# A two-layer encoder in split fp32: the gate and up products of one block of 128 output columns, ordered high parts first and low parts after

## The chip, the cores and the metric

The kernel runs on 1 core of one Trainium2 chip. The metric is device time: the median of 3 runs is 616.48 us (616.14 to 616.51). The engines are named as in the profile: PE (TensorE matmul), PEld (TensorE weight load), DVE (VectorE), ACT (ScalarE), POOL (GpSimd), SP (SyncE, which only issues DMAs here).

## The reference

Two layers of an encoder over 256 tokens of 1024 channels. Each layer has a mixer (three kinds of attention side by side) and a channel sublayer. Only the second one is touched here:

```python
D_MODEL, SEQ, DEPTH, D_FF = 1024, 256, 2, 2816
def channel_sublayer(x, n2, w_gu, cw, cb, w_dn):
    h = rms_norm(x, n2)
    g, u = jnp.split(h @ w_gu, 2, axis=-1)
    g = depthwise_conv_centred(g, cw, cb)        # along the tokens, 3 taps
    return x + (jax.nn.gelu(g, approximate=False) * u) @ w_dn
```

All tensors are float32. `h @ w_gu` is 256 x 1024 by 1024 x 5632.

## The kernel before

**Split numbers.** TensorE multiplies in the faster fp32r form. To keep accuracy, every operand is split into a high part (its fp32r rounding) and a low part (what is left). A product is then three products: high by high, low by high, high by low.

**Units of weights.** Weights come in units of at most 128 x 2048 values, 51 a layer. `load` (L581) brings a unit into one of four `raw` buffers by a DMA from SP's queue. `split` (L607) makes the two parts chunk by chunk: ACT casts a chunk of 512 columns into `wp_hi`, DVE subtracts and writes `wp_lo`; there are two buffers of each (`PARTS`). `unit` (L625) hands out the next unit and first records the loads four units ahead and the splits two units ahead.

**Gate and up.** `h2` (L1244, `act_hT` in the profile) holds the normalised input, transposed: for each of 8 groups of 128 channels the 256 tokens' high parts and beside them their 256 low parts. `half_up` (L1259) makes 256 output columns of gate or up from one unit. For each of its two blocks of 128 columns (`j`) it takes one PSUM bank (`psw_w`, four banks) of 128 x 512, and for each of 8 channel groups (`k`) `part` issues two matmuls: `wh` against all 512 columns of `h2[:, k]` (128x512: both tokens' parts at once), and `wl` against the 256 columns of the tokens' high parts (128x256, added to the first half of the bank). In the text the first is a wide product, the second a narrow one. Each has its own weight load. `joined` adds the bank's two halves: ACT copies the second half out, DVE adds the first. With `first=True`, the first gate unit of a layer, the order is written out by hand, because half of `h2` is still being made then.

**What follows.** `gate` (L1305) scales, convolves and applies GELU; `up` (L1324) multiplies and splits the result into `act_ch` and `act_cl`; `down` (L1334) multiplies these with `w_down` in 24 matmuls of 128x512 a unit, into four accumulators that stay in PSUM through the layer (`psa_a`). The sequence `FFN` (L74) is G0 U0 G1 D0 U1 G2 D1 U2 ... G10 U10 D9 D10. In layer 0, steps 4 to 9 also split the output projection's weights of layer 1 (`keep`, L565, tiles `act_mixT`) and store them to DRAM, and steps 2 to 4 make tables for layer 1.

**Order on the engines.** The code does not issue instructions directly: it records operations with a rank (its place in the program, plus some hundred for work that may come later). `order` (L303) then plays a list schedule: at each step it takes the ready operation that could start first by its own model of durations (`cost`, L416: an fp32r matmul of n columns is n / 2.4 + 2.5 ns), ties going to the lower rank, and this fixes each engine's instruction order. So a change of order in the program can shift neighbours on other engines. All instructions are issued from one place (L413), so the profile has L413 on every row, and groups are told apart by tiles.

Of the kernel before, what the change touches and what calls it, by code (L numbers as in the profile page):

```python
# [18 lines left out]
P = 128  # L19
# [3 lines left out]
KD = D // P  # L23
# [432 lines left out]
def encoder_kernel(  # L456
# [21 lines left out]
    nc = Plan(tc)  # L478
# [146 lines left out]
    def unit():  # L625

        i = taken[0]
        taken[0] += 1
        with nc.later(SPLIT_LATER):
            while len(raws) < min(i + AHEAD + RAWS - PARTS, len(views)):  # L630
                load(len(raws))
            while len(parts) < min(i + AHEAD, len(views)):
                split(len(parts))
        return parts[i]
# [14 lines left out]
    def split_T(srcs, hi, lo, k0, g, name):  # L649


        n = g.shape[1]
        for b in range(0, n, 2):
            m = min(2, n - b)
            ps = psw.tile([P, 2, S], F32, tag="w", name=f"pt_{name}_{b}")
            for i in range(m):
                k = b + i
                for t in range(NT):
                    nc.tensor.transpose(
                        ps[:, i, t * P : (t + 1) * P], srcs[t][:, k * P : (k + 1) * P], ident  # L660
                    )
            for i in range(m):
                k = b + i
                h, o = hi[:, k0 + k], lo[:, k0 + k]
                nc.scalar.activation(h, ps[:, i], AF.Copy, scale=g[:, k : k + 1])
                nc.vector.scalar_tensor_tensor(
                    o, ps[:, i], g[:, k : k + 1], h.bitcast(F32), ALU.mult, ALU.subtract
                )

    def halves(h):  # L670
        return [xs[:, t, h * 512 : (h + 1) * 512] for t in range(NT)]
# [144 lines left out]
    for l in range(DEPTH):  # L816
# [427 lines left out]
        h2 = act.tile([P, KD, 2, S], F32R, tag="hT", name=f"h2{l}", bufs=1)  # L1244
        h2_hi, h2_lo = h2[:, :, 0], h2[:, :, 1]
# [13 lines left out]
        def half_up(name, first=False):  # L1259

            wh, wl = unit()
            ps = [psw.tile([P, 2, S], F32, tag="w", name=f"{name}{j}") for j in range(2)]

            def part(j, k):
                js = slice(j * P, (j + 1) * P)
                nc.tensor.matmul(ps[j], wh[:, k, js], h2[:, k], start=k == 0, stop=False)
                nc.tensor.matmul(ps[j][:, 0], wl[:, k, js], h2_hi[:, k], start=False, stop=k == KD - 1)

            if first:
                for j in range(2):  # L1270
                    part(j, 0)
                split_T(halves(1), h2_hi, h2_lo, 4, gains[:, 2, l, 4:8], f"n2{l}1")
                for j in range(2):
                    for k in range(1, 4):
                        part(j, k)
                for k in range(4, KD):
                    part(0, k)
                for k in range(4, KD):
                    part(1, k)
                row_scale()  # L1280
                return ps
            for j in range(2):
                for k in range(KD):
                    part(j, k)
            return ps

        def row_scale():

            for t in range(NT):
                nc.tensor.transpose(  # L1290
                    rps[:, t * P : (t + 1) * P], r2[:, t : t + 1].to_broadcast([P, P]), ident
                )
            nc.vector.tensor_copy(rb, rps[:, :S])
# [11 lines left out]
        def gate(s):  # L1305
            nm = f"{l}_{s}"
            Gs = joined(half_up(f"G{nm}", s == 0), f"Gs{nm}")
            nc.vector.tensor_tensor(Gs, Gs, rb.unsqueeze(1).to_broadcast([P, 2, S]), op=ALU.mult)
            A = act.tile([P, 2, S], F32, tag="s2k", name=f"A{nm}", bufs=NS2K)
            for j in range(2):  # L1310
                f = 2 * s + j
                col = lambda i: cw[:, 22 * i + f : 22 * i + f + 1]
                nc.scalar.activation(A[:, j], Gs[:, j], AF.Identity, bias=col(3), scale=col(1))
                nc.vector.scalar_tensor_tensor(
                    A[:, j, 1:S], Gs[:, j, 0 : S - 1], col(0), A[:, j, 1:S], ALU.mult, ALU.add
                )
                nc.vector.scalar_tensor_tensor(
                    A[:, j, 0 : S - 1], Gs[:, j, 1:S], col(2), A[:, j, 0 : S - 1], ALU.mult, ALU.add
                )
            B = act.tile([P, 2, S], F32, tag="s2k", name=f"B{nm}", bufs=NS2K)  # L1320
            nc.scalar.activation(B, A, AF.Gelu)
            made[s] = B

        def up(s):  # L1324
            nm = f"{l}_{s}"
            C = joined(half_up(f"U{nm}"), f"C{nm}")
            nc.vector.tensor_tensor(C, made[s], C, op=ALU.mult)
            ch = act.tile([P, 2, S], F32R, tag="ch", name=f"ch{nm}", bufs=2)
            cl = act.tile([P, 2, S], F32R, tag="cl", name=f"cl{nm}", bufs=2)
            nc.scalar.copy(ch, C)  # L1330
            nc.vector.tensor_tensor(cl, C, ch.bitcast(F32), op=ALU.subtract)
            ready[s] = (ch, cl)
# [114 lines left out]
```

## Time and profile before

The profiled execution took 616.62 us, of which the span from its first to its last instruction is 614.9 us.

| | |
|---|---|
| median of the runs | 616.48 us |
| profiled execution, its span | 616.62 us, 614.9 us |
| granted TensorE clock, mean | 0.999 |
| HBM traffic | 196 GB/s over the span |
| DMA from `w_gate_up` | 44 issues of 1024 KB, 5.1 us to landing |

How to read it: a matmul's row in the timeline gives its start, and a duration that includes the time in the pipeline; since matmuls overlap, the pace is the distance from one start to the next, not the duration. A timeline row merges neighbours of the same kind (x2). PEld rows are weight loads; they overlap the matmuls. The clock times in the rows are counted from the span's start.

### The profile page before, as it was taken

The numbers are of one execution on the slowest core, as the hardware profiler recorded it, in microseconds if no ns is written. First come the engines' busy times: TensorE is split into PE (matmuls) and PEld (weight loads), VectorE is DVE, ScalarE is ACT, GpSimd is POOL, SyncE is SP. The second block draws the span as 40 slices with busy tenths as digits, with TensorE's granted clock in tenths as the row PEclk, the third lists the DMA queues.
The fourth block names the chain that finished last, engine by engine and source line by source line (L and its number), as shares of the span: only waits on it lengthen the run. The fifth ranks groups of instructions, "written<-read, shape, count | busy, mean of one in ns | idle before, by whom it ended". The sixth has DMA issues, their size and how long they took to land.

```text
span 614.9 us, 9864 instructions
## 1 busy us (share of the span) xinstructions
PE 605.8 (99%) x3484; PEld 523.8 (85%) x3484; DVE 487.4 (79%) x1000; ACT 428.1 (70%) x1064; POOL 82.5 (13%) x136
## 2 busy tenths in 40 slices
PE   8999999999999999999999999999999999999997
PEld 6998878888888888888899988887888888888885
DVE  4898989897777988887867797867977777777774
ACT  6788989686566676666588898866755656556651
POOL 2731230211400000000022212332000000000000
PEclk9999999999999999999999999999999999999999
DMA  8794312655596999978444744553565556555501
GB/s 279 273 290 156 102 36 86 227 191 194 169 244 237 366 350 325 312 272 277 154 151 153 243 136 173 201 179 119 200 228 174 173 202 203 173 176 202 187 20 68
DMA packets 85073, 121.44 MB, mean 198 GB/s; under 512 B 9864, under 2 KB 69608, under 8 KB 85024
## 3 DMA queue, kind: packets, MB, share of 16 engines
q1 hardware_dynamic: 82752, 112.17, 55.3%
q0 software_dynamic: 1728, 8.39, 3.8%
q8 instruction: 27, 0.44, 0.3%
q10 hardware_dynamic: 544, 0.26, 0.2%
q14 instruction: 22, 0.18, 0.1%
HBM read 110.93 MB, written 9.88 MB: 196 GB/s over the span
## 4 chain that ended last, share of the span: by engine, by line
PE 93%; DVE 2%; ACT 2%; issue 1%; DMA 1%; POOL 0%; SPq 0%; DVEq 0%; ACTq 0%
PE psw_w L413 50%; PE psa_a L413 43%; DVE const_x L413 1%; ACT act_s2k L413 1%; DMA wp_raw<-in_w_in_dram 1%; DVE act_hT L413 1%; ACT act_hT L413 1%; ACT wp_hi L413 0%; DVE wp_lo L413 0%; POOL small_rstd L413 0%; ACT act_mixT_hi L413 0%; POOL small_ms L413 0%; SPq L413 0%; DVE act_mixT_lo L413 0%; DVE small_ss L413 0%
## 5 line engine op out<-in xcount | busy, mean ns | idle before, releaser
L413 DVE TENSOR_TENSOR wp_lo<-wp_raw,wp_hi 128x512 fp32r<-128x512 f32 (+2 forms) x332 | 232.9, 732 | 43.8 <-ACT wp_hi L413 42.3
L413 PE MATMUL psw_w<-act_hT,wp_hi 128*128 128x512 f32 x704 | 248.6, 397 | 0.4 <-DVE act_hT L413 0.4
L413 ACT CAST wp_hi<-wp_raw 128x512 fp32r<-128x512 f32 (+2 forms) x332 | 203.2, 661 | 27.0 <-PE psw_w L413 15.5
L413 PE MATMUL psw_w<-act_hT,wp_lo 128*128 128x256 f32 x704 | 196.5, 280 | 0.0
L413 PEld LDWEIGHTS psw_w<-act_hT,wp_hi 128*128 128x128 f32 x704 | 132.0, 188 | 32.6 <-DVE act_hT L413 1.1
L413 PEld LDWEIGHTS psw_w<-act_hT,wp_lo 128*128 128x128 f32 x704 | 132.7, 189 | 1.1
L413 PE MATMUL psa_a<-wp_hi,act_hT 128*128 128x384 f32 (+2 forms) x448 | 112.8, 332 | 0.7 <-ACT act_hT L413 0.5
L413 ACT COPY act_s2k<-psw_w 128x256 f32<-128x256 f32 x88 | 32.3, 372 | 74.5 <-PE psw_w L413 74.5
L413 PEld LDWEIGHTS psa_a<-wp_hi,act_hT 128*128 128x128 f32 x448 | 77.9, 189 | 3.8 <-ACT act_hT L413 1.0
L413 PE MATMUL psa_a<-wp_lo,act_hT 128*128 128x384 f32 (+2 forms) x224 | 74.8, 335 | 0.0
L413 PE MATMUL psa_a<-wp_lo,act_ch 128*128 128x512 f32 x176 | 69.5, 395 | 0.0
L413 PE MATMUL psa_a<-wp_hi,act_ch 128*128 128x512 f32 x176 | 69.4, 394 | 0.0
L413 PE MATMUL psa_a<-wp_hi,act_cl 128*128 128x512 f32 x176 | 65.8, 394 | 0.0
L413 DVE TENSOR_TENSOR act_s2k<-psw_w,act_s2k 128x256 f32<-128x256 f32 x88 | 36.8, 422 | 30.1 <-ACT act_s2k L413 29.7
L413 PEld LDWEIGHTS psa_a<-wp_lo,act_hT 128*128 128x128 f32 x224 | 42.3, 189 | 2.3 <-DVE wp_lo L413 1.3
L413 PEld LDWEIGHTS psa_a<-wp_hi,act_cl 128*128 128x128 f32 x176 | 33.2, 188 | 7.8
L413 PEld LDWEIGHTS psa_a<-wp_hi,act_ch 128*128 128x128 f32 x176 | 33.1, 188 | 7.8
L413 PEld LDWEIGHTS psa_a<-wp_lo,act_ch 128*128 128x128 f32 x176 | 33.1, 188 | 6.9
L413 DVE SCALAR_TENSOR_TENSOR act_s2k<-act_s2k,act_cw,act_s2k 128x255 f32<-128x255 f32 x88 | 36.9, 478 | 1.5 <-ACT act_s2k L413 1.3
L413 POOL TENSOR_TENSOR small_rstd<-small_ms,const_mh 128x6 f32<-128x6 f32 (+2 forms) x26 | 31.4, 1208 | 2.2
L413 ACT ACTIVATE act_s2k<-act_s2k,act_cw 128x256 f32<-128x256 f32 x44 | 24.1, 595 | 10.0 <-DVE act_s2k L413 9.6
L413 PE MATMUL psw_w<-act_ch,const_v 128*128 128x256 f32 x128 | 28.6, 286 | 1.1 <-ACT act_s2k L413 1.1
(112 smaller groups left out, 779.1 us busy)
## 6 DMA issues: line engine op xcount, KB each, us to landing
wp_raw<-in_w_gate_up_dram SPq DMA_DIRECT2D x44, 1024.0 KB, 5.1
wp_raw<-in_w_down_dram SPq DMA_DIRECT2D x22, 1024.0 KB, 4.8
wp_raw<-in_w_in_dram SPq DMA_DIRECT2D x14, 768.0 KB, 5.5
wp_raw<-in_w_in_dram SPq DMA_DIRECT2D x8, 1024.0 KB, 5.6
wp_raw<-in_w_out_dram SPq DMA_DIRECT2D x8, 768.0 KB, 6.3
dram_khi<-act_mixT_hi SPq DMA_DIRECT2D x4, 768.0 KB, 4.4
dram_klo<-act_mixT_lo SPq DMA_DIRECT2D x4, 768.0 KB, 5.8
wp_lo<-dram_klo POOLq DMA_DIRECT2D x4, 768.0 KB, 4.8
```

What stands on the lines that cost most here:

```text
L413: getattr(o.engine.real, o.method)(*map(real, o.args), **{k: real(v) for k, v in o.kw.items()})
```

## The change

In every unit but the first gate unit of a layer, the 16 matmuls of a block of 128 columns are reordered: the eight with the weights' high parts first, then the eight with the low parts. No instruction is added or removed, and none changes its operands.

```diff
+            def large(j, k):
+                nc.tensor.matmul(ps[j], wh[:, k, j * P : (j + 1) * P], h2[:, k], start=k == 0, stop=False)
+
+            def little(j, k):
+                nc.tensor.matmul(
+                    ps[j][:, 0], wl[:, k, j * P : (j + 1) * P], h2_hi[:, k], start=False, stop=k == KD - 1
+                )
+
             def part(j, k):
-                js = slice(j * P, (j + 1) * P)
-                nc.tensor.matmul(ps[j], wh[:, k, js], h2[:, k], start=k == 0, stop=False)
-                nc.tensor.matmul(ps[j][:, 0], wl[:, k, js], h2_hi[:, k], start=False, stop=k == KD - 1)
+                large(j, k)
+                little(j, k)
...
             for j in range(2):
                 for k in range(KD):
-                    part(j, k)
+                    large(j, k)
+                for k in range(KD):
+                    little(j, k)
             return ps
```

In the order of the changed program, all 84 blocks concerned stand on PE as eight wide and eight narrow matmuls in a row; PE's other instructions keep their order but for a few neighbours among the `down` matmuls. On ACT, DVE and SP some tens of neighbouring instructions of the channel sublayer change places (casts of weight chunks against evictions of PSUM banks, one store of `act_mixT` against the load of a `w_down` unit).

## Prediction

> **What bounds the kernel now.** I read the page first (busy shares, then the chain that ended last), then the busy time by stage.
>
> ```profile
> span 614.9 us, 9864 instructions
> PE 605.8 (99%) x3484; PEld 523.8 (85%) x3484; DVE 487.4 (79%) x1000; ACT 428.1 (70%) x1064; POOL 82.5 (13%) x136
> ...
> PE 93%; DVE 2%; ACT 2%; issue 1%; DMA 1%; POOL 0%; SPq 0%; DVEq 0%; ACTq 0%
> ...
> 135.00:310.00 175.00, 175.00 (x914) 148.60 (x913) 143.58 (x242) 113.54 (x208) 10.12 (x18) 1.00 0.80 264
> 430.00:600.00 170.00, 170.00 (x902) 145.01 (x901) 130.03 (x222) 103.96 (x187) 0.00 (x0) 1.00 0.52 176
> ```
>
> The last two rows are the stretches in which the changed units run (columns: stretch, length, then PE, PEld, DVE, ACT, POOL busy, granted clock, DMA share, GB/s). PE is busy for all of both, at full clock; DVE has 31 and 40 us to spare, ACT 61 and 66. The 9 us in which PE idles lie elsewhere. So nothing can be won here by removing a wait: the time changes by the pace at which the same matmuls follow each other, or by a wait that does not exist yet.
>
> A busy PE does not show the pace; distances between starts do. These are rows of PE's timeline: first rows of units of layer 1, of two runs of narrow matmuls, and of two runs of wide ones.
>
> ```profile
> 437.18 0.40 PE L413 MATMUL psw_w<-act_hT,wp_hi 128*128 128x512 f32 x1
> ...
> 442.83 0.39 PE L413 MATMUL psa_a<-wp_hi,act_ch 128*128 128x512 f32 x1
> ...
> 448.40 0.39 PE L413 MATMUL psw_w<-act_hT,wp_hi 128*128 128x512 f32 x1
> ...
> 454.04 0.40 PE L413 MATMUL psw_w<-act_hT,wp_hi 128*128 128x512 f32 x1
> ...
> 465.26 0.40 PE L413 MATMUL psw_w<-act_hT,wp_hi 128*128 128x512 f32 x1
> ...
> 470.82 0.39 PE L413 MATMUL psw_w<-act_hT,wp_hi 128*128 128x512 f32 x1
> ...
> 599.48 0.40 PE L413 MATMUL psa_a<-wp_hi,act_ch 128*128 128x512 f32 x1
> ```
>
> ```profile
> 47.20 0.40 PE L413 MATMUL psa_a<-wp_hi,act_hT 128*128 128x256 f32 x2
> ...
> 51.88 0.41 PE L413 MATMUL psa_a<-wp_hi,act_hT 128*128 128x256 f32 x2
> ...
> 106.84 0.28 PE L413 MATMUL psw_w<-act_ch,const_v 128*128 128x256 f32 x1
> ...
> 107.53 0.38 PE L413 MATMUL psw_w<-const_ident,act_sqm 128*128 128x128 f32 x2
> ```
>
> ```profile
> 54.28 0.62 PE L413 MATMUL psa_a<-wp_hi,act_hT 128*128 128x512 f32 x2
> ...
> 55.87 0.39 PE L413 MATMUL psa_a<-wp_hi,act_hT 128*128 128x512 f32 x1
> ...
> 300.02 0.39 PE L413 MATMUL psa_a<-wp_hi,act_cl 128*128 128x512 f32 x1
> ...
> 305.85 0.40 PE L413 MATMUL psa_a<-wp_lo,act_ch 128*128 128x512 f32 x1
> ```
>
> From G1 (437.18) to D9 (599.48) stand ten gate units, ten up units and nine down units. D0, from 442.83 to 448.40, is 24 wide matmuls in 5.57 us: 232.1 ns each. The 20 units of gate and up have 16 pairs each, so a pair (wide, narrow) takes (162.30 - 9 x 5.57) / 320 = 350.5 ns on average. It is not one pace: U1 (448.40 to 454.04) has 5.64 us for 16 pairs, 352.5 ns; U2 (465.26 to 470.82) has 5.56, 347.5 ns. The same instructions, with PE never idle, run at two paces. That is the uncertainty of this forecast.
>
> **The change part by part.** It touches 42 units (44 without the two first gate units), 84 blocks, 672 pairs. Nothing is added or removed, weight loads and DMAs included.
>
> *Pace on PE, before:* 672 x 350.5 ns = 235.5 us. *After:* a wide matmul now follows a wide one, and a narrow one a narrow one. Wide in a row: 232.1 ns in D0, 233.2 ns in the later run (300.02 to 305.85, 25 steps), 227.1 ns in the early one (54.28 to 55.87, 7 steps). Narrow in a row: 120.0 ns in the projections (47.20 to 51.88, 39 steps), 115 ns in the attention (106.84 to 107.53, 6 steps). I take 232.1 for the wide ones, because the down units are their neighbours and have the same engines working beside them. For the narrow ones I take 118.4, which is what the present pair leaves for its narrow half (350.5 - 232.1) and lies between the two rows, nearer to the longer run. The sum is 672 x (232.1 + 118.4) = 235.5 us, so the change of pace comes to 0. Its bounds: 227.1 + 115 = 342.1 ns gives 672 x -8.4 = -5.6 us; 233.2 + 120.0 = 353.2 ns gives 672 x 2.7 = +1.8 us.
>
> *Weight loads.* Every matmul has one, and each narrow matmul is shorter than its load's row:
>
> ```profile
> L413 PEld LDWEIGHTS psw_w<-act_hT,wp_lo 128*128 128x128 f32 x704 | 132.7, 189 | 1.1
> ```
>
> If a load held the array for the whole 189 ns and only a wide matmul could cover it, eight narrow ones in a row would be slower. The run at 47.20 answers this: there each of the narrow matmuls has its load too, and they follow at 120.0 ns. I take 0.
>
> The Trainium skill, page "TensorE: Matmul & The Clock Gate", section "LDWEIGHTS (loading the stationary operand)", gives columns / 1.2, that is 107 ns for 128 columns, an estimate that a narrow matmul covers. By it the loads cost 0 in either order; by the row's 189 ns taken as occupancy the change would cost 47 us. The run at 120.0 ns agrees with the page, not with the row read as occupancy.
>
> *When the parts are needed.* The wide matmuls now reach the unit's last high chunk after 6 x 232 ns = 1.4 us instead of 6 x 350 = 2.1 us; the low parts are needed 1.9 us in instead of 0.2. For U1 of layer 1 these rows of ACT and DVE make the parts:
>
> ```profile
> 441.42 0.62 ACT L413 CAST wp_hi<-wp_raw 128x512 fp32r<-128x512 f32 x1
> 443.30 1.66 ACT L413 CAST wp_hi<-wp_raw 128x512 fp32r<-128x512 f32 x3
> ...
> 445.17 1.29 DVE L413 TENSOR_TENSOR wp_lo<-wp_raw,wp_hi 128x512 fp32r<-128x512 f32 x2
> ```
>
> The last high chunk is done at 444.96 and will be needed at 449.8: 4.8 us to spare. The low parts are done at 446.46, needed from 450.3. The tightest unit is U4 of layer 0, where DVE is still at the low parts when the unit starts:
>
> ```profile
> 197.44 4.29 DVE L413 TENSOR_TENSOR wp_lo<-wp_raw,wp_hi 128x512 fp32r<-128x512 f32 x7
> ...
> 198.08 0.62 PE L413 MATMUL psw_w<-act_hT,wp_hi 128*128 128x512 f32 x2
> 198.54 0.28 PE L413 MATMUL psw_w<-act_hT,wp_lo 128*128 128x256 f32 x1
> ```
>
> There the change lets the low parts come 1.4 us later. Both go at 0; the cover is the two units of run-ahead. No new wait is added.
>
> *Evictions and buffers.* A bank's last product is still a narrow one with k = 7, so ACT's copy and DVE's add start when they do now. The high buffer comes free 8 x 118 ns = 0.9 us earlier at the end of a unit. That can only shorten ACT's waits, which PE does not feel:
>
> ```profile
> ACT act_s2k L413 <- PE psw_w L413: 40.1, 39, 1.6
> ...
> ACT wp_hi L413 <- PE psw_w L413: 7.9, 10, 0.9
> ```
>
> The few neighbours that change places on ACT, DVE and SP move by one chunk (0.55 to 0.65 us each by the rows above) within that spare time; a load from SP that passes a store finds four raw buffers. 0, bounded by the 4.8 us of cover. POOL's queue keeps its order.
>
> **The sum.** 0 against the profiled 616.62 us (span 614.9 and 1.7 around it), which is 0.14 above the median of 616.48. I forecast 616.5 us.
>
> **The rivals.**
>
> *A: the runs fall into the quick pace.* Eight equal matmuls settle where the units at 347.5 ns or the runs at 227.1 and 115 ns are. For it: U2 shows that quick paces exist without any change of the work. Against: the down units, 24 wide in a row, stay near 232, and the longest narrow run stays at 120. If half the blocks find the quick pace of 342.1 ns, half of -5.6: 613.7 us; if all, 610.9.
>
> *B: the narrow run settles at 120.0 and the wide one at 233.2,* the paces of the longest runs, while today's quick units at 347.5 are lost. Its place is PE in every block, its price up to 672 x 2.7 ns: 618.3 us. It decides above 352.3 ns a pair, where 672 x 1.83 ns make 0.2%. For it: no long run of either kind in these rows is quicker than 232 or 120 once settled. Against: runs of eight may be too short to settle, and the narrow runs of the attention do not reach 120.
>
> *C: the weight loads are not covered in the narrow run.* 84 x 8 x (189 - 118.4) ns = 47 us: 663 us. Against it stands the run at 120.0; for it only that two of each three loads there bring the same columns. The same page, section "Back-to-back issue gap", says that the spacing is set by loads and matmuls together, pipelined through a window of 64; alternation would then let a wide matmul pay for a narrow one's load.
>
> *D: high chunks come too late.* If ACT's casts were just in time, four chunks at 0.55 us (2.2 us) would stand against 1.86 us of eight wide matmuls: 0.35 us in 42 units, 15 us: 631 us. Against it, the 4.8 us of cover.
>
> **How the numbers follow.** Forecast of no change 0.37, A 0.31, B 0.27, C 0.03, D 0.02. About 0.2%, 1.2 us, is what a measurement of this kernel can tell from no change. Faster by more is A: 0.31. Slower by more is B, C and D: 0.32. The rest is 0.37. The likeliest case's own range is 615.3 to 617.7. The range reaches to half of A with a little beyond, and to B: 613.2 to 618.4; it leaves out A in all blocks, C and D.
>
> **What would show it.** PE busy for the whole of both stretches again, with no wait on `wp_hi` or `wp_lo`: if not, D. The distance from the first wide to the first narrow matmul of a block, over eight: 232 by the forecast, 227 or less by A, 233 or more by B. The distance from the first narrow one to the next block, over eight: 118 by the forecast, 115 or less by A, 120 by B, 189 by C. The down units should stay at 5.57 us; if they move, the pace is carried from one unit into the next and the sum by blocks misses it. Wrong would be a block whose two runs don't resemble any run of the trace.

## The result and the profile after

The changed kernel takes 615.12 us (median of 18 runs, 614.23 to 615.77); the kernel before, run beside it, 616.11 us (18 runs, 615.25 to 616.66). The ratio is 0.9984, its 95% interval 0.9977 to 0.9992: faster by about 1.0 us, 0.16%. The forecast was no change, 616.5 us.

The page of the changed kernel, its span, its busy shares and the head of its chain:

```profile
span 614.0 us, 9882 instructions
...
PE 604.2 (98%) x3484; PEld 525.1 (86%) x3484; DVE 488.2 (80%) x1000; ACT 428.2 (70%) x1064; POOL 83.4 (14%) x136
...
PE 93%; ACT 2%; DVE 2%; issue 1%; DMA 1%; SPq 1%; POOL 0%; DVEq 0%; ACTq 0%
```

The same two stretches by busy time (stretch, length, then PE, PEld, DVE, ACT, POOL busy, granted clock, DMA share, GB/s):

```profile
135.00:310.00 175.00, 175.00 (x920) 149.78 (x919) 145.03 (x243) 113.95 (x210) 11.01 (x18) 1.00 0.80 264
430.00:600.00 170.00, 170.00 (x902) 146.05 (x902) 130.05 (x222) 105.28 (x189) 0.00 (x0) 1.00 0.53 175
```

And the waits of PE that the profile shows (us in total, times, the longest):

```profile
PE psw_w L413 <- ACT act_s2k L413: 1.7, 2, 1.1
PE psa_a L413 <- ACT act_hT L413: 1.3, 1, 1.3
PE psw_w L413 <- POOL const_warm L413: 1.0, 1, 1.0
PE psw_w L413 <- DVE const_x L413: 0.8, 2, 0.5
PE psw_w L413 <- DVE act_hT L413: 0.4, 1, 0.4
PE psw_w L413 <- DVE act_mixT_lo L413: 0.4, 1, 0.4
```

PE is busy in the whole of both stretches at full clock, as before, and it waits nowhere for `wp_hi` or `wp_lo`. The list of before has the same six rows, with 0.5 us for `act_hT` from ACT instead of 1.3 and the others within 0.1 us, so no wait has become shorter by as much as the gain. The chain has the same shape. So the gain is no removed wait; it is looked for in the pace, and that is read from the distances in PE's timeline of the changed kernel, layer 1:

```profile
442.29 0.39 PE L413 MATMUL psa_a<-wp_hi,act_ch 128*128 128x512 f32 x1
...
447.87 2.01 PE L413 MATMUL psw_w<-act_hT,wp_hi 128*128 128x512 f32 x8
449.71 1.12 PE L413 MATMUL psw_w<-act_hT,wp_lo 128*128 128x256 f32 x8
450.67 2.00 PE L413 MATMUL psw_w<-act_hT,wp_hi 128*128 128x512 f32 x8
452.51 1.11 PE L413 MATMUL psw_w<-act_hT,wp_lo 128*128 128x256 f32 x8
453.46 2.00 PE L413 MATMUL psw_w<-act_hT,wp_hi 128*128 128x512 f32 x8
...
598.66 0.39 PE L413 MATMUL psa_a<-wp_hi,act_ch 128*128 128x512 f32 x1
```

Since a row merges neighbours of one kind, a run of eight is now one row. Eight wide ones take 449.71 - 447.87 = 1.84 us, 230 ns each; eight narrow ones 450.67 - 449.71 = 0.96 us, 120 ns each. Both blocks of U1 take 2.79 to 2.80 us. D0, 442.29 to 447.87, still takes 5.58 us.

From the first row of D0 to the first row of D9 stand 19 of the changed units and nine down units: 598.66 - 442.29 = 156.37 us. Before it was 599.48 - 442.83 = 156.65 us, so 0.28 us less in this layer. Over the starts of all rows of the 42 units, the profiled execution of before has 235.80 us and that of after 234.88: 0.92 us less, about the difference of the two spans (614.9 and 614.0). The pair went from 235.80 / 672 = 350.9 ns to 349.5.

This is a balance of a gain and a loss. Before, 26 of the 42 units were slow (5.65 us on average) and 16 quick (5.55); after, all but the first of each layer take 5.59. By the starts in the two traces, the 26 together became 1.53 us shorter and the 16 became 0.60 us longer.

### The profile page after: what moved, and what is told of

Read it like the earlier page. It is cut to its first block, busy times and chain, and to the rows that moved or that the text cites. A ratio compares the mean times of both kernels' runs of the same rounds, so it can differ in the third digit from the quotient of the medians.

```text
span 614.0 us, 9882 instructions
## 1 busy us (share of the span) xinstructions
PE 604.2 (98%) x3484; PEld 525.1 (86%) x3484; DVE 488.2 (80%) x1000; ACT 428.2 (70%) x1064; POOL 83.4 (14%) x136
## 4 chain that ended last, share of the span: by engine, by line
PE 93%; ACT 2%; DVE 2%; issue 1%; DMA 1%; SPq 1%; POOL 0%; DVEq 0%; ACTq 0%
PE psw_w L413 50%; PE psa_a L413 43%; DVE const_x L413 1%; ACT act_s2k L413 1%; DMA const_x<-in_x_dram 1%; SPq L413 1%; ACT act_hT L413 1%; DVE act_hT L413 0%; ACT wp_hi L413 0%; DVE wp_lo L413 0%; POOL small_rstd L413 0%; ACT act_mixT_hi L413 0%; POOL small_ms L413 0%; DVE act_mixT_lo L413 0%; DVE small_ss L413 0%
## 5 line engine op out<-in xcount | busy, mean ns | idle before, releaser
L413 PE MATMUL psw_w<-act_hT,wp_hi 128*128 128x512 f32 x704 | 180.6, 394 | 0.4 <-DVE act_hT L413 0.4
L413 PEld LDWEIGHTS psw_w<-act_hT,wp_hi 128*128 128x128 f32 x704 | 127.9, 189 | 25.5 <-DVE act_hT L413 1.2
L413 PEld LDWEIGHTS psw_w<-act_hT,wp_lo 128*128 128x128 f32 x704 | 97.7, 190 | 6.9
L413 PE MATMUL psw_w<-act_hT,wp_lo 128*128 128x256 f32 x704 | 102.5, 283 | 0.0
L413 PE MATMUL psa_a<-wp_hi,act_cl 128*128 128x512 f32 x176 | 68.2, 395 | 0.0
L413 ACT ACTIVATE act_s2k<-act_s2k 128x512 f32<-128x512 f32 x22 | 13.9, 631 | 27.9 <-DVE act_s2k L413 27.9
```

Of the source, the lines that this page charges most:

```text
L413: getattr(o.engine.real, o.method)(*map(real, o.args), **{k: real(v) for k, v in o.kw.items()})
```

## The experiments

Each stands beside runs of the kernel before on its own chip. "Pair" is one wide and one narrow matmul. The stretch from D0 to D9 of layer 1 is used as the measure wherever the order of the units' matmuls leaves its ends in place.

### The order on PE alone, and the other engines alone

The change also moved some neighbours on ACT, DVE and SP. The first kernel takes the order planned for the kernel before and regroups only the matmuls of each block; the second takes the order planned for the changed kernel and puts the matmuls back into alternation. The lines that note which matmuls form a block, and in which order, are left out here.

```diff
-            for i in self.order():
+            for i in self.regrouped(self.order()):
```
```diff
+    def regrouped(self, done):
+        out, held = [], {}
+        for i in done:
+            block = self.blocks.get(i)
+            if block is None:
+                out.append(i)
+                continue
+            held.setdefault(id(block), []).append(i)
+            if len(held[id(block)]) == len(block):
+                out += block
+        return out
```

> The matmuls of a block grouped (eight wide, eight narrow), while ACT, DVE and SP keep the order that they had before the change. Theory O (the order of wide and narrow matmuls on PE alone sets the pace): every one of the 84 blocks takes 2.79 to 2.80 us as after the change, and the time is 0.7 to 1.2 us below before. Rival N (the neighbours that changed places on ACT, DVE and SP made the difference): the blocks keep the two paces of before, 2.77 to 2.78 and 2.81 to 2.83 us, and the time is within 0.3 us of before.

> Wide and narrow matmuls alternate as before, while ACT, DVE and SP have the order that they have after the change. Theory O: blocks at two paces again, 2.77 to 2.78 and 2.81 to 2.83 us, none at 2.79 to 2.80 throughout; time within 0.6 us of before (which share of the units falls to which pace is open). Rival N: blocks at 2.79 to 2.80 us, time 0.7 to 1.2 us below before.

The first took 615.25 us against 615.57, ratio 0.9994 (0.9985 to 1.0003). Its timeline, layer 1 (its line number differs, the rows are the same ones):

```profile
441.79 0.39 PE L427 MATMUL psa_a<-wp_hi,act_ch 128*128 128x512 f32 x1
...
447.37 2.01 PE L427 MATMUL psw_w<-act_hT,wp_hi 128*128 128x512 f32 x8
...
598.16 0.39 PE L427 MATMUL psa_a<-wp_hi,act_ch 128*128 128x512 f32 x1
```

598.16 - 441.79 = 156.37 us, and 234.88 us over the 42 units: to 0.01 us the figures of the changed kernel. So the order on PE alone sets the pace of the blocks; the neighbours' moves are not needed for it. The times alone would not have shown it: their interval includes 1.

The second took 710.08 us, ratio 1.152, and answers nothing. What PE waited for, foremost:

```profile
PE psw_w L427 <- ACT wp_hi L427: 72.6, 42, 3.3
```

A wide matmul held back to the place where its block's last matmul was planned stands behind the casts of a later unit into the same high buffer. So it multiplies that later unit's high parts (that part of the computation is changed), and waits for them: 42 waits, 72.6 us. The question that it was to answer is settled by the first kernel.

### Runs of sixteen

```diff
             for j in range(2):
                 for k in range(KD):
                     large(j, k)
+            for j in range(2):
                 for k in range(KD):
                     little(j, k)
```

> Runs twice as long: the 16 wide matmuls of both blocks of a unit, then the 16 narrow ones. After the change the wide matmuls of a run start at 236 ns and come down to 227 by the eighth, the narrow ones stand at 120 from the third on. Theory O with settling (a run settles, the wide one at 227, the narrow one at 120): the second eight wide take 8 x 227, a unit takes 5.57 us against 5.59, the time is about 0.9 us below that after the change. Rival S (a long wide run goes to the 232 ns of the down units): second eight wide 8 x 232, a unit 5.61 us, time about 1 us above that after the change.

It took 614.42 us against 615.57, ratio 0.9981 (0.9972 to 0.9990). Its timeline, layer 1:

```profile
441.29 0.39 PE L413 MATMUL psa_a<-wp_hi,act_ch 128*128 128x512 f32 x1
...
446.87 3.82 PE L413 MATMUL psw_w<-act_hT,wp_hi 128*128 128x512 f32 x16
450.53 2.08 PE L413 MATMUL psw_w<-act_hT,wp_lo 128*128 128x256 f32 x16
452.44 1.78 PE L413 MATMUL psw_w<-act_hT,wp_hi 128*128 128x512 f32 x7
...
597.28 0.39 PE L413 MATMUL psa_a<-wp_hi,act_ch 128*128 128x512 f32 x1
```

Sixteen wide ones take 450.53 - 446.87 = 3.66 us. The first eight took 1.84 us in the changed kernel, so the second eight take 1.82. The starts of the single matmuls in the traces (the timeline above merges them) show where the run settles. The table has the mean distance to the next start by place in the run, over all units:

| place | 1 | 2 | 3 | 4 | 5 | 6 | 7 | 8 | 9 to 16 |
|---|---|---|---|---|---|---|---|---|---|
| wide, runs of eight, ns | 235.7 | 233.1 | 229.2 | 233.3 | 229.9 | 228.0 | 228.0 | 226.6 | |
| wide, runs of sixteen, ns | 238.5 | 230.7 | 229.5 | 233.7 | 229.6 | 229.1 | 228.4 | 226.7 | 226.7 |
| narrow, runs of eight, ns | 113.1 | 119.1 | 120.2 | 120.1 | 119.7 | 120 | 120.4 | 119.9 | |
| narrow, runs of sixteen, ns | 113.3 | 119.2 | 120.0 | 120.0 | 120.0 | 120.0 | 120.0 | 120.0 | 120.0 |

(The rows of eight are from the changed kernel, those of sixteen from the repetition below.) A run of wide ones settles at 226.7 ns, one of narrow ones at 120.0. A run of eight wide ones spends most of itself on the way there: its eight places add to 1843.8 ns, 30 ns over eight settled ones. Halving the number of changes between the widths saves that once a unit, less the 7.6 ns by which a narrow run's first two places are short: 22 ns, and the units went from 5.589 to 5.569 us.

### Are the two paces of the alternation reset by four instructions?

Back to the kernel before, but each unit begins wide, wide, narrow, narrow.

```diff
                 for k in range(KD):
-                    part(j, k)
+                    if j == 0 and k < 2:
+                        if k == 0:
+                            large(0, 0)
+                            large(0, 1)
+                            little(0, 0)
+                            little(0, 1)
+                    else:
+                        part(j, k)
```

> Alternating as before, but each unit starts with two wide and two narrow matmuls and alternates from there. Theory C (alternation has two paces, and which one a unit takes is carried over from the matmuls before it): all units, given the same start, take one pace, all 5.55 us or all 5.64; in the first case the time is about 2.5 us below before, in the second about 1 us above. Rival (the pace belongs to the unit's buffers or to what the other engines do beside it): the units keep a mix of both paces, about 26 slow and 16 quick as before.

One run, 616.47 us. Its timeline, layer 1:

```profile
448.10 0.62 PE L413 MATMUL psw_w<-act_hT,wp_hi 128*128 128x512 f32 x2
...
459.38 0.40 PE L413 MATMUL psa_a<-wp_hi,act_ch 128*128 128x512 f32 x1
...
464.98 0.63 PE L413 MATMUL psw_w<-act_hT,wp_hi 128*128 128x512 f32 x2
...
476.10 0.39 PE L413 MATMUL psa_a<-wp_hi,act_ch 128*128 128x512 f32 x1
```

U1 and G2 take 11.28 us (448.10 to 459.38), U2 and G3 11.12 (464.98 to 476.10): both paces are still there and change from one down unit to the next. One pace for all units, as theory C had it, did not come. By itself this fits the rival too (a pace that belongs to the unit's buffers or its neighbours); if theory C holds, the four matmuls did not make the starts alike. The alternations entered from settled runs and the second execution of the kernel before, both below, tell more.

### Why do the down units stay at 232 ns?

Their 24 wide matmuls in a row do not settle at 226.7. The single starts in the changed kernel's trace show a repeating pattern instead: in its D0 and D1 of layer 1, from the third place on, the distances go 228, 230, 232, 241, 233, 231, 231 ns, within 2 ns, and begin again, 232 on average. Two kernels, both on top of the runs of sixteen, try their order: the first makes in each down unit first the 16 products with the high weights, then the eight with the low ones; the second keeps the order by accumulator but never uses the same `act_ch` twice in a row. Only the new loops are shown; `one` issues one matmul, with the high (0) or low (1) part of the activations by `a` and of the weights by `b`.

```diff
+            for t, h in accs:
+                for s in steps:
+                    for a in range(2):
+                        for j in range(2):
+                            one(t, h, s, j, a, 0, a == 0 and j == 0, False)
+            for t, h in accs:
+                for s in steps:
+                    for j in range(2):
+                        one(t, h, s, j, 0, 1, False, j == 1)
```
```diff
+            turns = [(0, 0, 0), (1, 0, 1), (0, 1, 0), (1, 1, 0), (0, 0, 1), (1, 0, 0)]
+            for t, h in accs:
+                for s in steps:
+                    for n, (j, a, b) in enumerate(turns):
+                        one(t, h, s, j, a, b, n == 0, n == 5)
```

> Runs of 16 in gate and up as in e3_runs16, and in the down units the 16 products with the weights' high parts first, then the 8 with the low parts; no two neighbours have the same stationary tile any more, and the moving tile changes from high to low once a unit. The down units were the rows from which the forecast took 232.1 ns for a wide matmul. Theory M (what keeps them at 232 is their own order: each stationary tile used twice running, or the moving tile changing between high and low parts): they come down to 227 ns, 5.44 us a unit, and the time is about 2.9 us below e3_runs16, 4 us below before. Rival L (232 belongs to the operands' places, weights moving and activations standing still): 5.57 us a unit, time as e3_runs16.

> Runs of 16 in gate and up as in e3_runs16; in the down units each accumulator's six products in an order in which no two neighbours have the same stationary tile, while the moving tile still changes between high and low parts. Within theory M: if the repeated stationary tile is what slows, the down units take 5.44 us as in e7_down_by_part; if it is the change of the moving tile between the two parts, 5.57 us. Rival L: 5.57 us in both.

The first took 617.62 us against 615.91, ratio 1.0032 (1.002 to 1.0043); the second 614.74, ratio 0.9979 (0.9970 to 0.9989), the gain of the runs of sixteen and no more. The timeline of the first, D0 of layer 1 and the two places where it waits:

```profile
302.41 1.19 PE L413 MATMUL psa_a<-wp_hi,act_ch 128*128 128x512 f32 x4 [1.30 <-ACT act_ch L413]
...
443.28 0.62 PE L413 MATMUL psa_a<-wp_hi,act_ch 128*128 128x512 f32 x2
...
448.86 3.82 PE L413 MATMUL psw_w<-act_hT,wp_hi 128*128 128x512 f32 x16
...
603.77 1.19 PE L413 MATMUL psa_a<-wp_hi,act_ch 128*128 128x512 f32 x4 [0.62 <-ACT act_ch L413]
```

D0 takes 448.86 - 443.28 = 5.58 us in the first, and in the second:

```profile
441.61 0.39 PE L413 MATMUL psa_a<-wp_hi,act_ch 128*128 128x512 f32 x1
...
447.19 1.09 PE L413 MATMUL psw_w<-act_hT,wp_hi 128*128 128x512 f32 x4
```

5.58 us again. Neither the order of the parts nor a repeated `act_ch` is the reason; theory M falls for these two orders. The pace is the one that rival L forecast, but the reason that L gives (the operands' places) was not tested by itself. The first kernel lost its time mostly at the end of each layer, where D9 and D10 share the order: their first high products now reach step 10's `act_ch` before ACT has made it. The two waits are 1.9 us of the 2.9 us between the two medians. What else sets the down units apart (they move weights over `act_ch` where gate and up move `h2` over weights, and they write other banks) was not tried separately and stays open.

### An alternation entered from settled runs

Two kernels keep an alternation and enter it always in the same way: after eight wide matmuls, or after eight wide and eight narrow ones. The new lines, which stand in place of the changed kernel's loops:

```diff
+            for k in range(KD):
+                large(0, k)
+            for k in range(KD):
+                little(0, k)
+                large(1, k)
+            for k in range(KD):
+                little(1, k)
```
```diff
+            for k in range(KD):
+                large(0, k)
+            for k in range(KD):
+                little(0, k)
+            for k in range(KD):
+                part(1, k)
```

> In each unit eight wide matmuls, then narrow ones of the first block and wide ones of the second in turn, then eight narrow ones. Theory C (the alternating order has two paces, and the state in which it is entered decides): entered from a settled wide run (227 ns) it goes at 346.7 ns a pair in every unit, and a unit takes 1.84 + 2.77 + 0.95 = 5.57 us. Rival (the alternation itself is slow half of the time, however it is entered): about half of the units at 353 ns a pair, 5.62 us, the others at 5.57.

> The first block of each of the 42 units runs eight wide and eight narrow matmuls as in the changed kernel, the second block alternates; so every alternation is entered from a settled narrow run, where the run with the wide run ahead entered it from a settled wide run and was slow (353 ns a pair) in all 42 units. Theory S (the state at entry decides, and the narrow run leaves the good one): all 42 second blocks run quick, 2.77 us, units 2.80 + 2.77 = 5.57 us, their sum about 233.9 us, and one pace everywhere. Rival T (an alternation after any settled run is slow): all 42 second blocks 2.82 us or more, units 5.62, sum 236.0. Rival V (the entry does not decide, the earlier run was chance): both paces appear among the 42 blocks.

One run each: 617.05 and 617.45 us. The timeline of the first, layer 1:

```profile
448.53 2.01 PE L413 MATMUL psw_w<-act_hT,wp_hi 128*128 128x512 f32 x8
...
459.77 0.39 PE L413 MATMUL psa_a<-wp_hi,act_ch 128*128 128x512 f32 x1
...
465.35 2.01 PE L413 MATMUL psw_w<-act_hT,wp_hi 128*128 128x512 f32 x8
...
476.59 0.39 PE L413 MATMUL psa_a<-wp_hi,act_ch 128*128 128x512 f32 x1
```

Two units take 11.24 us after D0 and 11.24 after D1; all 42 units are alike within 5 ns but for the first of each layer, and the alternating part of every one has 353 ns a pair. The 346.7 ns that theory C expected did not come, and neither did the rival's mix. The timeline of the second:

```profile
443.14 0.40 PE L413 MATMUL psa_a<-wp_hi,act_ch 128*128 128x512 f32 x1
...
448.74 2.01 PE L413 MATMUL psw_w<-act_hT,wp_hi 128*128 128x512 f32 x8
...
454.37 1.99 PE L413 MATMUL psw_w<-act_hT,wp_hi 128*128 128x512 f32 x8
456.20 1.11 PE L413 MATMUL psw_w<-act_hT,wp_lo 128*128 128x256 f32 x8
457.15 0.40 PE L413 MATMUL psw_w<-act_hT,wp_hi 128*128 128x512 f32 x1
...
459.98 0.40 PE L413 MATMUL psa_a<-wp_hi,act_ch 128*128 128x512 f32 x1
```

The grouped block of G2 takes 457.15 - 454.37 = 2.78 us, the alternating one 459.98 - 457.15 = 2.83, and so it is in 41 of the 42 units (2.72 us in U4 of layer 0, one of whose wide matmuls stands in the block ahead). So entered from a settled run, of either width, an alternation takes the slower pace, and it does so in every unit but that one: this is theory T in the words of the second kernel's expectation. Theory S, that narrow runs leave a better start, was wrong, and so was rival V, that the entry does not decide.

What ran before counts for runs of one width, too. U1's grouped block, which follows D0, takes 2.80 us by the single starts; G2's, which follows an alternation, 2.78, because its wide run is at 226 to 227 ns from its second place on, where that of U1 wanders between 225 and 236. And D0 now takes 448.74 - 443.14 = 5.60 us, as do all 18 down units that stand alone (5.601 to 5.602), where they have 5.576 in the changed kernel. Their distances go 238 and 229 ns in turn here, 233.4 on average, not by the pattern of seven.

### The kernel before, once more

No edit; only a second execution.

> The kernel before the change once more. If the two paces of its units are set by the program and not by chance, the same units as in the first profile are slow (5.64 us) and quick (5.55 us), and the 42 units sum to 235.8 us within 0.1. If the mix changes from execution to execution, the sum can lie anywhere between 233.5 and 237.0, and the gain of the change is only what this execution's mix made it.

One run, 615.12 us, span 613.3. Its timeline, layer 1:

```profile
441.67 0.39 PE L413 MATMUL psa_a<-wp_hi,act_ch 128*128 128x512 f32 x1
...
447.24 0.40 PE L413 MATMUL psw_w<-act_hT,wp_hi 128*128 128x512 f32 x1
...
458.35 0.39 PE L413 MATMUL psa_a<-wp_hi,act_ch 128*128 128x512 f32 x1
...
463.91 0.39 PE L413 MATMUL psw_w<-act_hT,wp_hi 128*128 128x512 f32 x1
...
475.20 0.39 PE L413 MATMUL psa_a<-wp_hi,act_ch 128*128 128x512 f32 x1
...
598.03 0.39 PE L413 MATMUL psa_a<-wp_hi,act_ch 128*128 128x512 f32 x1
```

U1 and G2 take 11.11 us, 347.2 ns a pair; U2 and G3 11.29, 352.8 ns. In the first execution it was the other way round: U1 slower, U2 quicker. The same program in another execution has its two paces in other units, so they belong neither to a unit's buffers nor to its order of instructions.

The traces also show a sign of what is handed on. In layer 1 of both executions, each of the nine down units D0 to D8 takes either 5.56 us (5.562 to 5.563) or 5.58 us (5.577 to 5.578). After the first kind the next units are slow, after the second kind quick, 18 times out of 18. D0 is of the first kind in one execution and of the second in the other; from there on slow and quick change at every down unit. This fits a pace that depends on the state in which PE comes to the alternation, a state that passes through a down unit. What set D0 apart was not found, and whether the other engines have a part in it was not tested. From D0 to D9 it takes 598.03 - 441.67 = 156.36 us here, against 156.65 there; over the 42 units 235.21 against 235.80. So what the change gains in the units is 0.92 us against the one execution and 0.33 against the other, which has 22 quick units instead of 16. Had all 42 been quick (5.55 us), the grouped order at 5.59 would be the slower one by about 1.6 us; this is an estimate from these unit times, no execution showed it.

### The changed kernel and the runs of sixteen on one chip

> The changed kernel again, beside the one with runs of sixteen, on one chip. If a block's time is set by the order on PE alone, its 42 units sum to 234.88 us within 0.05 in this execution too, where the kernel before had 235.2 and 235.8 in two executions; ratio to before 0.9984, 0.9975 to 0.9995.

> Runs of sixteen again, beside the changed kernel. By the settled paces (226.7 and 120.0 ns) its 42 units are 0.84 us shorter than the changed kernel's, so its median should stand 0.6 to 1.0 us below it, a ratio to before of about 0.997. If the gain in the units is given back elsewhere, the two medians agree within 0.3 us.

The kernel before took 615.84 us (20 runs), the changed one 615.16 (11 runs), ratio 0.999 (0.9981 to 0.9998), the runs of sixteen 614.33 (10 runs), ratio 0.9975 (0.9966 to 0.9985). The first and the last row of the stretch in layer 1, of the changed kernel:

```profile
441.91 0.39 PE L413 MATMUL psa_a<-wp_hi,act_ch 128*128 128x512 f32 x1
...
598.28 0.39 PE L413 MATMUL psa_a<-wp_hi,act_ch 128*128 128x512 f32 x1
```

and of the runs of sixteen:

```profile
441.31 0.39 PE L413 MATMUL psa_a<-wp_hi,act_ch 128*128 128x512 f32 x1
...
597.30 0.39 PE L413 MATMUL psa_a<-wp_hi,act_ch 128*128 128x512 f32 x1
```

The changed kernel has 156.37 us for the third time (with the regrouped one), and 234.88 us over its 42 units. Runs of sixteen have 155.99 us as in their first execution; 0.38 us less in 19 units is 0.84 us in 42, and the medians stand 0.83 us apart. The two intervals overlap by a little, but the trace and the medians agree: runs of sixteen are quicker than both kernels.

## Why the prediction was wrong

**What bounds the kernel** was right: PE busy throughout, no wait to gain or to lose, a change of pace and nothing else (the grouped order on PE alone gave the whole pace of the changed kernel). Of the named signs, PE's busy time and the absence of waits on `wp_hi` and `wp_lo` came as said. The wide distance came at 230 ns, between the forecast's 232 and A's 227, and the narrow one at 119 to 120 instead of 118. The down units stayed near 5.57 us, but went from 5.56 or 5.58 to 5.576 throughout. That is 0.06 us over nine of them, nothing in the sum; but it is the sign that the prediction itself had named for a pace that is carried from one unit into the next, and the later runs bear it out.

**The pace after** is the step that failed: the narrow matmul was put at "118.4, which is what the present pair leaves for its narrow half (350.5 - 232.1)". A sum of 232.1 and what the present pair leaves beside it is the present pair, whatever the wide pace is; so that sum could give nothing but 0, and it carried no information from the trace. The two terms by themselves were off in opposite directions: the wide one, taken from the down units, at 232.1 against 230.5 measured (the eight places of the table), the narrow one at 118.4 against 119.1. Together about 349.5 instead of 350.5: 672 x -1.0 ns = -0.7 us, most of what was measured. The down units were the wrong neighbours to take the wide pace from: wide matmuls of gate and up settle at 226.7 ns, and the down units do not, in any of the three orders tried. The early run of 7 (227.1 ns), named as the lower bound, was the right row for the settled pace; that eight matmuls after a change of width do not reach it showed in no row of before.

**The base** was the other weak point. "350.5" was measured in one layer of one execution, in which the two paces had one mix; over all units that execution has 350.9, another 350.0. About half a nanosecond either way, 0.3 us, is not the kernel's but the execution's. The prediction saw the two paces and called them its uncertainty, but treated their mean as fixed. It also put at 0.2% what a measurement can tell from no change; the interval of the ratio is 0.08% to either side, so 0.16% stands clear of it.

**Weight loads, due times, buffers**: 0, as said. Eight narrow matmuls in a row, with a load each, follow at 120 ns in the changed kernel, so loads of 189 ns by their row do not hold PE up for as long as that. The estimate of 107 ns worked out from the Trainium skill, page "TensorE: Matmul & The Clock Gate", section "LDWEIGHTS (loading the stationary operand)", agrees with that.

**The rivals.** A, the quick pace, had the right direction, in part by luck: eight equal matmuls do move towards a settled pace, but eight are too few to get there (230.5, not 227.1), and the narrow ones settle at 120, not at 115. Of its price of 5.6 us for all blocks, 0.7 came. The grouped pair of 349.5 ns is not even as quick as the quick pair of before, 347; the time fell because each of the many slow units of before gained more (about 0.06 us) than a quick one lost (0.04). B had the narrow run right at 120.0 and the wide one wrong at 233.2. C and D did not happen: the narrow distance is 120, not 189, and PE waits for no chunk of the weights in the changed units.

The time lies in the range of 613.2 to 618.4 and 0.2 us under the likeliest case's own range; what was missed is a gain of 1.0 us that was put at nothing. How much of it is the change's stays uncertain: the units give 0.33 to 0.92 us by the execution compared, and the three comparisons of one and the same order on PE gave 1.0, 0.3 and 0.7 us.

## What to carry to other kernels

Where PE is never idle, read the pace as a distance between starts, for each kind of run by itself, and take both halves of a new order from rows; a remainder of the old order brings the old answer back. In gate and up, equal matmuls in long runs settled and kept one pace, while an alternation of widths ran at two; so rarer changes of width were worth 0.06 to 0.25% here, and one profiled execution is no fixed base for an alternating kernel. Differences of some tenths of a microsecond could be placed here because the stretch between two named rows repeats to 0.01 us in the grouped kernels; in the alternating one it moved by 0.29 us.

## What the runs showed of the hardware

The same alternating matmuls, with PE never idle and at full clock, run at about 347 or about 353 ns a pair. The two paces sit in other units from one execution of the same program to the next. What ran before the alternation counts: it is 353 ns in 42 of 42 units after a settled wide run and in 41 of 42 after a settled narrow run, and in layer 1 of the kernel before a down unit of 5.56 us was followed by slow units and one of 5.58 us by quick ones, 18 times out of 18. The quick pace is close to the sum of the two settled ones, 226.7 + 120.0 = 346.7 ns.

The Trainium skill, page "TensorE: Matmul & The Clock Gate", section "Back-to-back issue gap", gives columns / 2.4 + 2.5 ns for the gap of a single matmul, so 216 and 109 ns for 512 and 256 columns, and 131 ns for sustained matmuls of 512 columns. Both settled paces here lie about 11 ns above the first figures, and the wide one far above the 131 ns; here the measurement decides.

The 24 wide matmuls of a down unit take 5.576 us in the changed kernel, 5.56 or 5.58 us in the kernel before and 5.60 us where a grouped and an alternating block stand before them. What state it is that is carried over was not found.
